# Gate and output products of a hybrid layer moved from eight plain to seven half products over two blocks

## The chip, the cores and the metric

The kernel runs on one core of a Trainium2 chip. The metric is the device time of one execution in microseconds. A core has a matrix engine (PE; its weight loads are listed as PEld), a vector engine (DVE), a scalar engine (ACT), a general engine (POOL) and a sequencer that issues the DMA transfers (SP). Each engine works through its own list of instructions in order and waits on semaphores for the others. SBUF is the on-chip memory of 128 partitions, PSUM the eight banks that PE writes, DRAM the memory behind the DMA engines.

## The reference

One layer over 2048 tokens of width 1024, all in float32:

```
xn = RMSNorm(x)
aq ak av mq mk mv mo i f ga gm = split(xn @ w_in)        # 512 each, i f 4 each, ga gm 1024 each
A = chunked band attention(aq, ak, av)                   # 2048 x 512
M = sigmoid(mo) * headnorm(mLSTM(conv(mq, mk), mv, i, f))  # 2048 x 512
y = sigmoid(ga) * (A @ w_att_proj) + sigmoid(gm) * (M @ w_mlstm_proj)
x = x + y @ w_out
x = x + relu(RMSNorm(x) @ w_up)^2 @ w_down               # 1024 -> 4096 -> 1024
out = RMSNorm(x)
```

## The kernel before

**Blocks, spans, products.** The tokens are four blocks of 512 (b = 0 to 3); two blocks make a span (s = 0, 1). Every operand of a product is split into a rounded fp32r part and a rest, and each 128 x 128 x 512 product is three matmuls (`mm3`): high x high, high x low, low x high. A weight tile holds 128 x 1024 numbers, split by one ACT copy (line 332) and one DVE subtraction (line 334) into one of three slots `wsp`; a plain tile feeds 8 such triples, 24 matmuls. The raw tile is loaded by SP into one of four `wraw` slots.

**A block, plain products.** `dense` sends 60 weight tiles per block through PE: 4 for the attention values (`evac_v`), a small product for the gates i, f (line 484), 4 for mv (`evac_mv`), then four times q, k, mq, mk, mo (`evac_q`, `evac_k`, two `evac_conv`, `evac_og`), 8 for ga (`evac_ga`), 8 times gm and the two projections together (`evac_gm`, `evac_y`), and 8 for the output product (`evac_x2`). Attention and the mLSTM recurrence (the mixers) run on all engines beside these tiles. Attention goes by heads in pairs: a pair needs four `r` slots for its q and k; a head is two units of 256 tokens (scores line 842, exponential 857, transposes 873, their split 876 and 878, the product with v on line 807, the split of the result ending on line 824). The pool `sc` holds two units, the pool `pt` the transposed tiles of one, the pool `bias` two heads.

**A span, seven half products.** After two blocks, the feed-forward layer runs over the 1024 tokens of the span by Winograd's form of Strassen's scheme: blocks of tokens are the one halving, halves of the features the other, and seven products replace eight. `quad` does one such group: seven weight tiles, each used for two output tiles, 168 matmuls on line 460, where a plain form would take 192. The weight sums that it needs are built by DVE in the first span (`quad_w`, four subtractions of 128 x 1024 a group), kept in DRAM and loaded in the second. The seven sums of the activations are made by DVE, sent to DRAM (`ud`), loaded again and split into 28 `r` slots (`take_u`, split on lines 643 and 645). `after_up` adds up the products, `spread` makes the sums for the next product, `after_down` accumulates into 16 tiles.

**Pools and order.** `r` has 28 slots of two 128 x 512 tiles, `temp` 6 tiles, `ctx` 12, `sc` 4, and four tiles hold mv. A planner written into the kernel (`Flow`) fixes the order: every piece of work is a Python generator that says what it waits for, which pool it takes from and how long it takes on which engine; the planner emits by its own clock, and prefers the lower priority number among equals. Dense products may hold at most four PSUM banks that wait for their copy:

```
        if kind == "dense":
            if room < n or pool.held + n > 4:
                return False, None
```

The instructions of an engine are then put in their last order by the tile framework, which takes the emitted order as priority and lets an instruction go ahead when what it needs is there.

The lines that the change touches are in `dense`, `loader`, `quad`'s neighbours, `attention`, `recurrence`, the evacuation functions and the pools.

Of the kernel before, what the change touches and what calls it, by code (L numbers as in the profile page):

```python
# [25 lines left out]
P = 128  # L27
# [14 lines left out]
N_W = 60  # L42
N_Q = 16
# [157 lines left out]
class Layer:  # L201
# [6 lines left out]
    def make_tiles(self, pool, psum):  # L208
# [9 lines left out]
        self.ctx = Pool([f32(f"ctx{i}", 516) for i in range(12)])  # L218
        self.mvflat = [f32(f"mv{i}", 516) for i in range(NT)]
        self.mv = [m.rearrange("p (h c) -> p h c", h=MH) for m in self.mvflat]  # L220
# [73 lines left out]
    def loader(self):  # L294
        fl, io = self.fl, self.io
        i = 0
        for s in range(NS):
            for n in range(2 * N_W):
                (raw,) = yield "get", self.wraw, 1
                fl.spawn(self.split_w(i, io["w"][n % N_W], raw), 0)  # L300
                i += 1
            for q in range(N_Q):
                if s == 0:
                    raws, evs = [], [Event() for _ in range(4)]
                    fl.spawn(self.quad_w(i, q, raws, evs), 0)
                    for n in range(4):
                        (raw,) = yield "get", self.wraw, 1
                        raws.append(raw)
                        fl.spawn(self.load_w(io["wf"][q, n], raw, evs[n]), 0)
                else:  # L310
                    wf, td = io["wf"][q], self.td[q].ap()
                    for n, src in enumerate((wf[0], wf[2], td[0], td[1], wf[3], td[2], td[3])):
                        (raw,) = yield "get", self.wraw, 1
                        fl.spawn(self.split_w(i + n, src, raw), 0)
                i += 7

    def load_w(self, src, raw, ev):
# [4 lines left out]
    def split_w(self, i, src, raw):  # L322
        yield "sp", 1750, 2000
        self.nc.sync.dma_start(raw, src)
        yield from self.split_now(i, raw)
        self.fl.put(self.wraw, raw)

    def split_now(self, i, raw):
        fl, nc = self.fl, self.nc
        (w,) = yield "get", self.wsplit, 1  # L330
# [106 lines left out]

    def quad(self, A, aev, after, release):
# [28 lines left out]
    def dense(self):  # L467
        fl = self.fl
        for b in range(NB):
            B = self.blk[b]  # L470
# [6 lines left out]
            yield from self.token_tiles(xs, xe, lambda t, bk: self.evac_v(b, t, bk))  # L477

# [8 lines left out]
            none = [None] * KT  # L487
            yield from self.token_tiles(xs, none, lambda t, bk: self.evac_mv(b, t, bk))
            self.banks.want = 2
            for j in range(4):  # L490
                for which, fn in (("q", self.evac_q), ("k", self.evac_k)):
                    (bk,) = yield from self.feature_tile(xs, none)
                    fl.spawn(fn(b, j, bk), 1)
# [3 lines left out]
            for j in range(8):  # L497
                (bk,) = yield from self.feature_tile(xs, none)
                fl.spawn(self.evac_ga(b, j, bk), 1)
            if b % 2 == 0:  # L500
                fl.spawn(self.norm_in(b + 1), 3)
            self.banks.want = 3
            for j in range(8):
                (bg,) = yield from self.feature_tile(xs, none)
                fl.spawn(self.evac_gm(b, j, bg), 1)
                (ba, bm) = yield from self.feature_tile(B["mix"], B["mix_ev"], parts=2)
                fl.spawn(self.evac_y(b, j, ba, bm), 1)
            yield "wait", B["mix_ev"]
            fl.put(self.rpool, *B["mix"], *xs)
            fl.set(B["merged"])  # L510
            if b % 2 == 1:
                s = b // 2
                U, D = self.operands(), [self.operands() for _ in range(4)]
                fl.spawn(self.take_hn_early(s, *U), 2)
                for k in range(4):
                    fl.spawn(self.take_hn_late(s, k, *U), 1)
            for j in (0, 4, 1, 5, 2, 6, 3, 7):
                (bk,) = yield from self.feature_tile(B["y"], B["y_ev"])
                fl.spawn(self.evac_x2(b, j, bk), 1)
            fl.put(self.rpool, *B["y"])  # L520
            fl.spawn(self.norm_mid(b), 2)
            if b % 2 == 0:
                continue

            self.banks.want = 0
            if b + 1 < NB:
                fl.spawn(self.norm_in(b + 1), 3)
            for i in range(8):
                yield from self.quad(*U, self.after_up(s, i), release=i == 7)
                if i == 6:  # L530
                    fl.spawn(self.take_u(s, D), 2)
            fl.spawn(self.final(s), 2)
            self.mv_left = list(self.mvflat)
# [10 lines left out]
    def norm_in(self, b):  # L544
# [43 lines left out]
        if b % 2 == 1:  # L588
            yield "wait", [self.blk[b - 1]["merged"]]
        elif b > 0:  # L590
# [35 lines left out]
    def scale_in(self, b, k, slot, bk, dst, ev):  # L626
# [9 lines left out]
        fl.set(ev)  # L636
        yield from self.split(x, dst)
        fl.put(self.ctx if b == 0 else self.sc, slot)
        fl.set(self.blk[b]["xn"][k])

    def split(self, src, dst):
        yield "act", act_ns(T)
        self.nc.scalar.copy(dst[:, 0], src)  # L643
        yield "dve", dve_ns(T)
        self.nc.vector.tensor_sub(dst[:, 1], src, dst[:, 0].bitcast(F32))  # L645


    def attention(self, b):
        fl, B = self.fl, self.blk[b]
        pt = yield "get", self.rpool, 3  # L650
        self.pt = Pool(pt)
# [3 lines left out]
        for j in range(4):  # L655
            (B["mix"][j],) = yield "get", self.rpool, 1
            if b > 0:
                (vo,) = yield "get", self.rpool, 1
                yield "sp", 900, 2000
# [12 lines left out]
        fl.put(self.rpool, *pt)  # L672
        fl.put(self.rpool, *B["v"])

    def evac_v(self, b, t, bk):
# [10 lines left out]
        if b + 1 < NB:  # L686
            yield "sp", 900, 2000
            nc.sync.dma_start(self.vdram[b].ap().bitcast(F32)[t],
                              B["v"][t].rearrange("p a c -> p (a c)").bitcast(F32))

# [39 lines left out]
    def head(self, b, h):  # L730
        fl, nc, B = self.fl, self.nc, self.blk[b]
        k, q = B["kq"][h]
        if b > 0:
            yield "sp", 900, 2000
# [18 lines left out]
        if B["heads_left"][h // 2] == 0:  # L753
            if b > 0:
                fl.put(self.rpool, B["vo"][h // 2])
            fl.set(B["mix_ev"][h // 2])
        fl.set(B["head_done"][h])

    def unit(self, b, h, u, k, q, bias, done):
# [24 lines left out]
        slots = yield "get", self.pt, len(pieces)  # L784
# [26 lines left out]
        fl.put(self.pt, *slots)  # L811
# [71 lines left out]
    def gates(self, b, bk):  # L883
        fl, nc, B, sm = self.fl, self.nc, self.blk[b], self.sm
        V = nc.vector
        (tmp,) = yield "get", self.temp, 1
# [100 lines left out]
    def recurrence(self, b):  # L987
        fl, B = self.fl, self.blk[b]
        for h in range(MH):
            B["ctx"][h] = yield "get", self.ctx, 6  # L990
            fl.set(B["ctx_ev"][h])
            fl.spawn(self.rec_head(b, h), 1)

    def evac_mv(self, b, t, bk):
        fl, nc, B = self.fl, self.nc, self.blk[b]
        if b % 2 == 0 and b > 0:
            yield "wait", [self.acc_free[b // 2 - 1]]
        yield "pool", 120
        nc.gpsimd.memset(self.mv[t][:, :, 128:129], 1.0)
        yield "act", act_ns(512, True)  # L1000
        nc.scalar.copy(self.mv[t][:, :, 0:128], bk.rearrange("p (h c) -> p h c", h=MH))
# [9 lines left out]
    def evac_conv(self, b, h, which, bk):  # L1011
        fl, nc, B = self.fl, self.nc, self.blk[b]
        yield "wait", [B["ctx_ev"][h]]
        dst = B["ctx"][h][which][:, :512]
# [34 lines left out]
    def rec_head(self, b, h):  # L1049
# [3 lines left out]
        ex, mv, cst = self.ex, self.mv, self.cst[h]  # L1053
# [30 lines left out]
        yield "wait", B["mv_ev"]  # L1084
        (hs,) = yield "get", self.hs, 1
# [49 lines left out]
        fl.set(B["mix_ev"][4 + h])  # L1135
# [15 lines left out]
    def evac_ga(self, b, j, bk):  # L1151
        fl, nc, B = self.fl, self.nc, self.blk[b]
        (g,) = yield "get", self.ctx, 1
        yield "act", act_ns(512, True)
        nc.scalar.activation(g[:, :512], bk, AF.Tanh, scale=0.5)
        fl.put_dense(self.banks, bk)
        B["ga"][j] = g
        fl.set(B["ga_ev"][j])

    def evac_gm(self, b, j, bk):  # L1160
        fl, nc, B = self.fl, self.nc, self.blk[b]
        (g,) = yield "get", self.temp, 1
        yield "act", act_ns(512, True)
        nc.scalar.activation(g[:, :512], bk, AF.Tanh, scale=0.5)
        fl.put_dense(self.banks, bk)
        B["gm"][j] = g
        fl.set(B["gm_ev"][j])

    def evac_y(self, b, j, ba, bm):
        fl, nc, B = self.fl, self.nc, self.blk[b]  # L1170
        yield "wait", [B["ga_ev"][j], B["gm_ev"][j]]
        ga, gm = B["ga"][j], B["gm"][j]
        a, m = ga[:, :512], gm[:, :512]
        yield "dve", dve_ns(512)
        nc.vector.scalar_tensor_tensor(a, a, 1.0, ba, op0=ALU.add, op1=ALU.mult)
        fl.put_dense(self.banks, ba)
        yield "dve", dve_ns(512)
        nc.vector.scalar_tensor_tensor(m, m, 1.0, bm, op0=ALU.add, op1=ALU.mult)
        fl.put_dense(self.banks, bm)
        yield "dve", dve_ns(512)  # L1180
        nc.vector.tensor_add(a, a, m)
        fl.put(self.temp, gm)
        (r,) = yield "get", self.rpool, 1
        yield "act", act_ns(512)
        nc.scalar.copy(r[:, 0], a)
        yield "dve", dve_ns(512)
        nc.vector.tensor_sub(r[:, 1], a, r[:, 0].bitcast(F32))
        fl.put(self.ctx, ga)
        B["y"][j] = r
        fl.set(B["y_ev"][j])  # L1190

    def evac_x2(self, b, j, bk):
        fl, nc, B = self.fl, self.nc, self.blk[b]
        if j == 0:
            (B["tot"],) = yield "get", self.ctx, 1
        (x,) = yield "get", self.temp, 1
        x5 = x[:, :512]
        yield "sp", 900, 2000
        nc.sync.dma_start(x5, self.io["xt"][b, j])
        yield "dve", dve_ns(512)  # L1200
        nc.vector.scalar_tensor_tensor(x5, bk, 0.5, x5, op0=ALU.mult, op1=ALU.add)
        fl.put_dense(self.banks, bk)
        kept = Event()
        fl.spawn(self.store(self.x2d[b].ap()[j], x5, kept), 1)
        (h,) = yield "get", self.ctx, 1
        yield "act", act_ns(512, False, 1)
        nc.scalar.mul(h[:, :512], x5, self.gcol[:, 1, j:j + 1])
        if b % 2 == 0:
# [485 lines left out]
```

## Time and profile before

| what | value |
|---|---|
| time, median of 3 runs | 2928.76 us (2927.49 to 2929.96) |
| time of the profiled execution | 2927.55 us |
| its span, first to last instruction | 2925.3 us |
| PE busy | 2889.1 us (99%), 13952 matmuls |
| DVE busy | 1949.4 us (67%) |
| ACT busy | 1496.0 us (51%) |
| DMA | 468.31 MB, mean 160 GB/s |

The profile is one execution; the rows give a line of the kernel, an engine, an operation, how often it ran, how long all of them kept the engine busy and the mean of one. A matmul's own duration (390 ns) contains the time it spends in the array beside the next one; how fast they follow each other is read from a stretch of time and the count of matmuls in it. The time outside the span is 2.25 us.

### The profile page before, as it was taken

To read this page: it belongs to the slowest core of one execution; us is meant where nothing else is said; L and a number is where in the kernel's file an instruction comes from. 1 tells how busy PE (TensorE), PEld (TensorE's weight loads), DVE (VectorE), ACT (ScalarE), POOL (GpSimd) and SP (SyncE) were. 2 spreads that over 40 slices of the span, in tenths; PEclk is the share of its full clock that TensorE was granted. 3 is DMA by queue.
4 is the path that set the end of the run, shared out by engine and by line. 5 is a ranking of instruction groups with operands and counts; after the bars stand their busy time and mean duration, and the time that the engine had idled before them with its cause. 6 is when DMAs were issued, how large, how long until landed. Compare 5 with 4: busy or idle time off the path is not lost.

```text
span 2925.3 us, 38512 instructions
## 1 busy us (share of the span) xinstructions
PE 2889.1 (99%) x13952; PEld 2417.2 (83%) x13952; DVE 1949.4 (67%) x3609; ACT 1496.0 (51%) x2580; POOL 53.5 (2%) x124
## 2 busy tenths in 40 slices
PE   7999999999999999999999999999999999999998
PEld 6888888888888888888888888888888888888887
DVE  5785456985585557898758854569845744468775
ACT  4664344664365556444546652456633655564444
POOL 0000000000000000000000000000000000000000
PEclk9999999999999999999999999999999999999999
DMA  5333363323465558675542234532224655587652
GB/s 170 100 93 127 112 217 120 104 72 119 138 215 206 208 209 307 232 245 194 177 157 93 89 117 123 199 101 79 64 86 141 213 187 193 196 287 233 216 177 87
DMA packets 187967, 468.31 MB, mean 160 GB/s; under 512 B 21248, under 2 KB 27520, under 8 KB 187776
## 3 DMA queue, kind: packets, MB, share of 16 engines
q1 hardware_dynamic: 187776, 465.86, 48.3%
q8 instruction: 109, 1.79, 0.3%
q14 instruction: 82, 0.67, 0.1%
HBM read 339.95 MB, written 125.83 MB: 159 GB/s over the span
## 4 chain that ended last, share of the span: by engine, by line
PE 87%; DVE 7%; ACT 2%; issue 2%; DMA 1%; POOL 0%; SPq 0%; POOLq 0%; ACTq 0%; DVEq 0%
PE bank L460 39%; PE bank L393 13%; PE bank L394 13%; PE bank L395 13%; PE bank L807 2%; PE bank L873 1%; PE bank L842 1%; DVE wsp L334 1%; DVE sc L848 1%; DVE ctx L1029 1%; ACT wsp L332 1%; ACT sc L857 1%; DVE r L645 1%; PE bank L484 1%; DVE r L878 0%
## 5 line engine op out<-in xcount | busy, mean ns | idle before, releaser
L460 PE MATMUL bank<-r,wsp 128*128 128x512 f32 x5376 | 1227.8, 390 | 2.1 <-DVE ctx L1344 1.1
L460 PEld LDWEIGHTS bank<-r,wsp 128*128 128x128 f32 x5376 | 1006.5, 188 | 213.8 <-DVE ctx L1344 2.0
L332 ACT CAST wsp<-wraw 128x1024 fp32r<-128x1024 f32 x464 | 487.9, 1051 | 742.0 <-PE bank L460 256.0
L334 DVE TENSOR_TENSOR wsp<-wraw,wsp 128x1024 fp32r<-128x1024 f32 x464 | 567.2, 1222 | 410.7 <-ACT wsp L332 406.3
L393 PE MATMUL bank<-r,wsp 128*128 128x512 f32 x1664 | 662.3, 398 | 2.7 <-DVE tmp L819 2.0
L395 PE MATMUL bank<-r,wsp 128*128 128x512 f32 x1664 | 649.1, 390 | 0.0
L394 PE MATMUL bank<-r,wsp 128*128 128x512 f32 x1664 | 648.8, 390 | 0.0
L395 PEld LDWEIGHTS bank<-r,wsp 128*128 128x128 f32 x1664 | 312.3, 188 | 67.1
L393 PEld LDWEIGHTS bank<-r,wsp 128*128 128x128 f32 x1664 | 313.0, 188 | 61.5 <-DVE tmp L819 2.8
L394 PEld LDWEIGHTS bank<-r,wsp 128*128 128x128 f32 x1664 | 313.3, 188 | 56.8
L643 ACT CAST r<-tmp 128x512 fp32r<-128x512 f32 x264 | 162.3, 620 | 125.7 <-PE bank L460 50.6
L645 DVE TENSOR_TENSOR r<-tmp,r 128x512 fp32r<-128x512 f32 x264 | 177.7, 687 | 50.7 <-ACT r L643 50.1
L857 ACT ACTIVATE sc<-sc,scs 128x640 f32<-128x640 f32 (+4 forms) x128 | 97.3, 761 | 88.7 <-DVE scs L854 84.8
L1477 DVE TENSOR_TENSOR ctx<-bank,ctx 128x512 f32<-128x512 f32 x136 | 93.1, 685 | 46.1 <-PE bank L460 45.8
L1344 DVE TENSOR_TENSOR ctx<-bank,ctx 128x512 f32<-128x512 f32 x96 | 66.2, 689 | 85.4 <-PE bank L460 84.1
L848 DVE CUSTOM_DVE_ANT_0 sc<-bank,bias 128x320 f32<-128x320 f32 (+3 forms) x240 | 102.9, 462 | 24.3 <-PE bank L842 23.7
L807 PEld LDWEIGHTS bank<-r,r 128*128 128x128 f32 x672 | 98.6, 189 | 12.6 <-DVE r L878 3.5
L807 PE MATMUL bank<-r,r 128*128 128x256 f32 (+1 forms) x672 | 105.1, 278 | 1.9 <-DVE r L878 1.9
L393 PE MATMUL bank<-wsp,r 128*128 128x512 f32 x256 | 102.9, 402 | 1.5 <-ACT r L643 1.5
L1336 ACT ACTIVATE ctx<-ctx 128x512 f32<-128x512 f32 x96 | 60.6, 632 | 83.7 <-DVE ctx L1344 83.7
L394 PE MATMUL bank<-wsp,r 128*128 128x512 f32 x256 | 100.5, 393 | 0.0
L395 PE MATMUL bank<-wsp,r 128*128 128x512 f32 x256 | 99.5, 392 | 0.0
(217 smaller groups left out, 2725.2 us busy)
## 6 DMA issues: line engine op xcount, KB each, us to landing
wraw<-in_w SPq DMA_DIRECT2D x240, 512.0 KB, 3.5
wraw<-in_wf SPq DMA_DIRECT2D x112, 512.0 KB, 3.9
tmp<-u SPq DMA_DIRECT2D x224, 256.0 KB, 3.9
wsum<-wraw SPq DMA_DIRECT2D x64, 512.0 KB, 3.1
u<-ctx SPq DMA_DIRECT2D x128, 256.0 KB, 2.4
wraw<-wsum SPq DMA_DIRECT2D x64, 512.0 KB, 3.4
u<-tmp SPq DMA_DIRECT2D x96, 256.0 KB, 2.6
sc<-in_xt SPq DMA_DIRECT2D x48, 256.0 KB, 3.2
```

Of the source, the lines that this page charges most:

```text
L332: nc.scalar.copy(w[:, 0], raw)
L334: nc.vector.tensor_sub(w[:, 1], raw, w[:, 0].bitcast(F32))
L393: mm(ps, lh, rh, start=first, stop=False)
L394: mm(ps, lh, rl, start=False, stop=False)
L395: mm(ps, ll, rh, start=False, stop=last)
L460: mm(ps, wv[:, x, k, n], a[:, y], start=new and k == 0 and x == y == 0, stop=k == 3 and x == 1, skip_group_check=True)
L643: self.nc.scalar.copy(dst[:, 0], src)
L645: self.nc.vector.tensor_sub(dst[:, 1], src, dst[:, 0].bitcast(F32))
L807: nc.tensor.matmul(bk[:, c0:c0 + w], st, sl[:, x, o:o + w], start=n == 0, stop=n == total - 1)
L848: nc.vector.tensor_tensor_reduce(out=e[:, x * w:x * w + w], in0=bks[x][:, :w], in1=br[:, j0 + x * w:j0 + x * w + w], op0=ALU.add, op1=ALU. ...
L857: nc.scalar.activation(e[:, :n], e[:, :n], AF.Exp, scale=-1.0, bias=mx, accum_out=st[:, 2:3])
L1477: nc.vector.tensor_add(a, ps, a)
```

## The change

The products for ga and gm and the output product leave the plain tiles of a block and become groups of seven half products over a span: four groups for the gates (two output quarters, each for ga and gm), two for the output product, ahead of the eight and eight of the feed-forward layer. The plain tiles of a block are then 28 (v, q and k of all heads, mv, and four times mq, mk, mo) and 8 for the two projections, which `pair_tile` does for both blocks of the span after the second block's 28 tiles. Within a block the q and k tiles of all four pairs come right behind v.

What goes with it:

- The two mixers of the even block now run beside the odd block's 28 tiles. The even block's mixed tiles go to DRAM (`mixed`) and come back for the projections (`reload_mix`); the normalized input goes to DRAM too (`xnd`) and comes back as the operand sums of the gate groups (`take_xn`). The next block's normalization (`norm_in`) starts six tiles before the end of the even block's 28.
- A projection's result is copied from PSUM to DRAM (`evac_proj`) and loaded again behind each gate tile (`after_gate`), where the gate is applied and ga's and gm's parts are added. The sums of y go through DRAM to the output groups, and those of the normalized x to the first feed-forward groups, by `spread` and `take`, as the feed-forward layer did before between its two halves.
- The 36 plain weight tiles are split once; the split pair (1 MB) is kept in DRAM (`keep_w`) and loaded in all later uses (`reload_w`), so that 108 of 144 plain tiles need no ACT and DVE work.
- The pool `ctx` has 16 tiles, and the four tiles of mv come out of it.

The core of the diff:

```
-N_W = 60
-N_Q = 16
+N_IN = 28
+N_W = 36
+N_G, N_O, N_F = 4, 2, 8
+N_Q = N_G + N_O + 2 * N_F
...
+            for h in range(2):
+                plain += [(n, 2 * s + h == 0) for n in range(N_IN)]
+            for h in range(2):
+                plain += [(n, s == 0 and h == 0) for n in range(N_IN, N_W)]
+            for n, first in plain:
+                if first:
+                    (raw,) = yield "get", self.wraw, 1
+                    fl.spawn(self.split_w(i, io["w"][n], raw, n), 0)
+                else:
+                    w = yield from self.slot_w(i)
+                    fl.spawn(self.reload_w(i, n, w), 0)
...
+    def pair_tile(self, srcs, evs):
...
+        for n in range(2):
+            got += (yield "dense", self.banks, 1)
+            for k in range(4):
...
+                self.mm3(got[-1], wv[:, 0, k, n], wv[:, 1, k, n], srcs[k][:, 0], srcs[k][:, 1], k == 0, k == 3)
...
             yield from self.token_tiles(xs, xe, lambda t, bk: self.evac_v(b, t, bk))
+            self.banks.want = 3
+            for j in range(4):
+                for fn in (self.evac_q, self.evac_k):
+                    (bk,) = yield from self.feature_tile(xs, none)
+                    fl.spawn(fn(b, j, bk), 1)
...
             for j in range(4):
-                for which, fn in (("q", self.evac_q), ("k", self.evac_k)):
...
+                if b % 2 == 0 and j == 2:
+                    fl.spawn(self.norm_in(b + 1), 3)
                 for fn in (self.evac_conv_q, self.evac_conv_k, self.evac_og):
...
-            for j in range(8):
-                (bk,) = yield from self.feature_tile(xs, none)
-                fl.spawn(self.evac_ga(b, j, bk), 1)
...
+            fl.spawn(self.reload_mix(b - 1), 1)
+            for h in range(2):
+                e = b - 1 + h
+                M = self.blk[e]
+                if h == 1:
+                    G = self.operands()
+                    for k in range(4):
+                        fl.spawn(self.take_xn(s, k, *G), 2)
+                yield "wait", [M["mix_slots"]]
+                for x in range(2):
+                    for j in range(4):
+                        bks = yield from self.pair_tile(M["mix"][4 * x:4 * x + 4], M["mix_ev"][4 * x:4 * x + 4])
+                        for n in range(2):
+                            fl.spawn(self.evac_proj(s, h, x, 2 * j + n, bks[n]), 1)
...
+            for i in range(N_G):
+                yield from self.quad(*G, self.after_gate(s, i), release=i == N_G - 1)
+                if i == N_G - 2:
+                    O = self.operands()
+                    fl.spawn(self.take(self.yd.ap(), self.y_ev[s], 0.5, *O), 2)
+            self.tots = yield "get", self.bias, 2
+            for i in range(N_O):
+                yield from self.quad(*O, self.after_out(s, i), release=i == N_O - 1)
+                if i == N_O - 2:
+                    U = self.operands()
+                    fl.spawn(self.take(self.hd.ap(), self.h_ev[s], 1.0, *U), 2)
...
+        def finish(n, which, t, ps):
...
+            nc.scalar.activation(t5, t5 if ps is None else ps, AF.Tanh, scale=0.5)
...
+            nc.sync.dma_start(a[:, :512], self.projd.ap()[2 * h + x, j])
+            yield "dve", dve_ns(512)
+            nc.vector.scalar_tensor_tensor(t5, t5, 1.0, a[:, :512], op0=ALU.add, op1=ALU.mult)
```

`spread(tiles, evs, dst, out, k)` stores a11, a12 and a22 as they come, takes three `temp` tiles once a21 is there, makes s1, s2, s4 and the last difference with four DVE operations, and gives the tiles back when all seven stores have landed. `take(src, evs, scale, A, aev)` goes through the 28 operands of a group in order (the seven sums outside, the four k tiles inside): it waits for the store, loads a `temp` tile, takes an `r` slot and splits.

644 lines of the change are left out of this document (366 added, 278 removed).

## The prediction

> **What bounds the kernel now.** I read the page first, then the busy times by stretches, then single lines. On the page:
>
> ```profile
> span 2925.3 us, 38512 instructions
> PE 2889.1 (99%) x13952; PEld 2417.2 (83%) x13952; DVE 1949.4 (67%) x3609; ACT 1496.0 (51%) x2580; POOL 53.5 (2%) x124
> PE 87%; DVE 7%; ACT 2%; issue 2%; DMA 1%; POOL 0%; SPq 0%; POOLq 0%; ACTq 0%; DVEq 0%
> L460 PE MATMUL bank<-r,wsp 128*128 128x512 f32 x5376 | 1227.8, 390 | 2.1 <-DVE ctx L1344 1.1
> L332 ACT CAST wsp<-wraw 128x1024 fp32r<-128x1024 f32 x464 | 487.9, 1051 | 742.0 <-PE bank L460 256.0
> L334 DVE TENSOR_TENSOR wsp<-wraw,wsp 128x1024 fp32r<-128x1024 f32 x464 | 567.2, 1222 | 410.7 <-ACT wsp L332 406.3
> L645 DVE TENSOR_TENSOR r<-tmp,r 128x512 fp32r<-128x512 f32 x264 | 177.7, 687 | 50.7 <-ACT r L643 50.1
> L643 ACT CAST r<-tmp 128x512 fp32r<-128x512 f32 x264 | 162.3, 620 | 125.7 <-PE bank L460 50.6
> L1344 DVE TENSOR_TENSOR ctx<-bank,ctx 128x512 f32<-128x512 f32 x96 | 66.2, 689 | 85.4 <-PE bank L460 84.1
> ```
>
> PE is the bound: 99% busy and 87% of the chain that ended last. The 464 weight splits of DVE and ACT mostly wait for PE, not the reverse. By stretches (us, then busy us and instructions of PE, PEld, DVE, ACT, POOL, clock, DMA share, GB/s): the last tiles of a block, the feed-forward groups, and the in-projection of blocks 1 and 2 with its mixers.
>
> ```profile
> 730.00:830.00 100.00, 100.00 (x443) 82.78 (x442) 57.97 (x73) 41.04 (x57) 0.00 (x0) 1.00 0.52 166
> 930.00:1030.00 100.00, 100.00 (x443) 82.81 (x442) 59.28 (x68) 53.52 (x77) 0.00 (x0) 1.00 0.56 203
> 530.00:630.00 100.00, 98.73 (x575) 86.19 (x574) 87.48 (x232) 66.25 (x142) 3.77 (x11) 1.00 0.30 93
> 1530.00:1630.00 100.00, 99.26 (x592) 87.55 (x590) 88.62 (x244) 66.31 (x148) 4.88 (x14) 1.00 0.31 98
> ```
>
> Plain tiles and half products run at the same pace: 443 matmuls in 100 us, 0.2257 us each, at full clock. So fewer matmuls are time won, if PE stays fed. It nearly always is; the price of the change is where it isn't.
>
> **The gain.** Per block, ga, gm and out take 24 plain tiles of 24 matmuls; four blocks make 2304. Per span there are now six groups of 168, for two spans 2016. The 288 that vanish are worth 288 x 0.2257 = 65.0 us. Everything else PE does stays: the projections have 384 matmuls a span in both forms.
>
> **DVE and ACT.** Weight splits fall from 464 to 344 (36 plain, 308 for groups): DVE -120 x 1.222 = -147 us, ACT -126 us. Twenty-four weight sums in the first span add some 29 us to DVE. For the 128 x 512 operations I count 264 on DVE and 188 on ACT per span now (operand splits and sums, gates, additions of products, spreads, half of the 32 projection copies), against 140 and 108: +248 x 0.69 = +171 us and +160 x 0.62 = +99 us. DVE ends near 2000 us, ACT near 1470: neither becomes a bound over the whole span. Since PE hardly waits for weight splits now, their removal itself is priced at nothing; it makes room in the in-projection.
>
> **q and k first.** These rows are block 1: v copies, q evacuations, scores (128 matmuls are 16 units of 8), unit ends, the og tiles that end the in-projection, and the last recurrence transposes.
>
> ```profile
> L681 ACT CAST r<-bank x4: 583/589/589, 433.4 to 438.5; 128x512 fp32r<-128x512 f32 x4
> L702 DVE SCALAR_TENSOR_TENSOR r<-bank,r x8: 665/684/694, 474.3 to 610.4; 64x512 fp32r<-64x512 f32 x8
> L842 PE MATMUL bank<-r,r x64: 303/309/391, 481.6 to 557.2; 128*128 128x320 f32 x64
> L842 PE MATMUL bank<-r,r x80: 303/309/391, 481.6 to 580.2; 128*128 128x320 f32 x80
> L824 ACT CAST r<-tmp x16: 399/404/412, 500.0 to 690.7; 64x256 fp32r<-64x256 f32 x16
> L1043 ACT ACTIVATE ctx<-bank x4: 592/614/628, 502.7 to 641.8; 128x512 f32<-128x512 f32 x4
> L1125 PE MATMUL bank<-const,ctx x16: 270/272/327, 530.8 to 678.4; 128*128 128x128 f32 x16
> 410.00:642.00 232.00, 230.60 (x1254) 196.31 (x1253) 172.26 (x466) 133.71 (x280) 6.06 (x17) 1.00 0.35 111
> ```
>
> Units end every (690.7 - 500.0)/15 = 12.7 us. The q/k tiles of four pairs used to come spread over 136 us (474.3 to 610.4); now eight tiles of 24 x 0.2257 = 5.42 us come in 43. The 28 `r` slots hold xs 8, pt 3, v 4 and six per pair (mix, old v, four q/k): two pairs and one slot. So pair 3's q and k wait in their banks until older q/k slots have been read for the last time. In an even block that is when the scores of units 0 to 7 are done (557.2 - 474.3 = 83 us behind the first q), in an odd block, where mix isn't given back, those of units 0 to 9 (106 us). Behind them queue the four mv banks: only four dense banks may wait, so mv's third stands. PE gets there after 12 tiles (65.0), the 16 gate matmuls (3.6), 12 of mv (2.7) and, as I estimate from the mixers' surplus below, some 20 us of theirs, at about 91 us; the first q, the fifth tile, is copied at about 29. Pair 3's banks come free at 29 + 83 + 5 = 117 or 29 + 106 + 5 = 140 us: 26 or 49 us of standing, of which a third is filled by the mixers' own matmuls (575 against 443 in 100 us, smaller ones). Idle 17 or 33 us at the old pace, 83 us for blocks 1 to 3, the upper end. The lower end is nothing: DVE loses 28 x 1.22 = 34 us of the 172 it worked in such a block, and units that end every 9 us would close the gap. I take 2 us for block 2, 7 each for blocks 1 and 3: 16 us; block 0 has shorter units and no old v: 0.
>
> **Norm of the odd block.** Its squares and loads in block 2's case:
>
> ```profile
> L566 ACT ACTIVATE sc<-sc x8: 631/632/636, 672.5 to 692.0; 128x512 f32<-128x512 f32 x8
> L564 SPq DMA_DIRECT2D sc<-in_xt x8: 327/328/382, 669.0 to 687.7; - x8
> ```
>
> 23 us from first load to last square, then the small matmuls and the scaling, some 30 us in all. It begins six tiles (33 us, with mixers about 45) ahead of need, but its `sc` slots come behind the units that wait. Attention, begun 25 us earlier than before, should end about when the 28 tiles do (before: 49 us after og). Bounds 0 and 2 x 25; I take 3, since a stand at mv gives attention time.
>
> **Projections: DMA.** The issue rows (KB each, us to landing), one row of the timeline for a hand-over between engines (0.21 us idle), and two stretches with full queues:
>
> ```profile
> wraw<-in_w SPq DMA_DIRECT2D x240, 512.0 KB, 3.5
> tmp<-u SPq DMA_DIRECT2D x224, 256.0 KB, 3.9
> u<-ctx SPq DMA_DIRECT2D x128, 256.0 KB, 2.4
> u<-tmp SPq DMA_DIRECT2D x96, 256.0 KB, 2.6
> 404.84 1.23 DVE L334 TENSOR_TENSOR wsp<-wraw,wsp 128x1024 fp32r<-128x1024 f32 x1 [0.21 <-ACT wsp L332]
> 1115.00:1135.00 20.00, 19.62 (x87) 15.96 (x86) 14.13 (x19) 15.04 (x27) 0.00 (x0) 1.00 0.90 318
> 1155.00:1175.00 20.00, 20.00 (x90) 16.55 (x89) 14.04 (x17) 5.77 (x7) 0.00 (x0) 1.00 0.90 323
> ```
>
> 16 projection tiles take PE 384 x 0.2257 = 86.7 us. In that time the first span moves, in MB: weights 4.2 raw, 8.4 kept, 8.4 loaded; mix 4.2; projection stores 8.4; xn loads 4.2; first raw gate weights 2.1: 39.9. The second span moves 35.7 (16.8 of weights loaded, none kept). A share of 0.90 at 318 to 323 GB/s makes some 355 GB/s at a full share: 112 and 101 us, 26 and 14 more than PE's. Weights run two tiles ahead (10.8 us) and half of the mix loads (6 us) can go before the stage: 26 - 17 = 9 us and nothing. Bounds 0 and 40; I take 9.
>
> The Trainium skill, "DMA: Bandwidth & Descriptors", section Bandwidth, gives 425 GB/s for a 16 MB transfer by one core alone, and its note sets an HBM limit of about 358 GB/s against that. By 425 the stage would need 94 and 84 us, so this term would be nothing and the sum 9 us lower; the trace here, at 0.90 share and 323 GB/s, lies nearer the 358.
>
> **Gates to out, out to feed-forward.** The third product of a group needs s1 of the last a21 of the group before. Chain behind the gates: tanh 0.62, gate and addition 2 x 0.69, s1 0.69, store 2.6, load 3.9, split 0.62 + 0.69, which is 10.5, eight hand-overs at 0.21 and one more store (2.4) until the neighbour's three `temp` tiles are back: 14.6 us. Cover: two products, 48 x 0.2257 = 10.8. Late by 3.8; behind out, with one operation less, by about 2.8: 13 us for two spans. DVE is full there: per span the out groups have 14 weight splits (17.1), 28 product additions (19.3), 14 additions of squares (9.6), 8 spread operations (5.5), 28 operand splits (19.2) and in the first span 8 sums (9.8): 80.5 us against 2 x 168 x 0.2257 = 75.8. The 4.7 over goes on top: 18. Bounds: 0, if the emitted order lets s1 go first, and 45 (13 + 5, doubled by transfers as slow as 0.90 share makes them, and 9 for the takes behind).
>
> **Reload of mix, take of xn.** A mix tile needs one load (a raw weight of the same size: 3.5 us) and its slot is old; the xn operands have 43 us for 28 splits and 16 sums, 30 us of DVE. Late at most by one load each: bounds 0 and 14; I take 1 us each, 4 in all. Recurrence heads now come 3 tiles apart instead of 5, with two at a time; head 3 ended 678.4 - 641.8 = 37 us after og, and 43 us of even projections stand before that is needed: nothing, and 10 if it slips. The start gets the xn stores and 1 MB stores on SP's queue; block 0's stretch is far below full share: nothing.
>
> **Sum.** -65.0 + 16 + 3 + 9 + 18 + 4 = -15. The profiled execution took 2927.55 us (2.25 outside the span), 1.2 under the median shown, so the forecast is 2912.6, rounded to 2913.
>
> **Rivals.** (1) The gain is eaten: each cost comes a third dearer than taken, 50 x 1.3 = 65, result 2922 to 2934. For it: five new places, each short; against it: the same kind of hand-over through DRAM between up and down costs PE nearly nothing today (2.1 us before 5376 matmuls on line 460). (2) Slower, by the banks held for pair 3: attention keeps its 12.7 us a unit, PE idles 83 us instead of 16 in blocks 1 to 3, 67 more: 2980. Units at 12 us or slower decide it; break-even comes at 31 us of idling. For it: the slot count and the queue of four; against it: DVE loses a fifth of its work there, and PE, while standing, runs the units' own matmuls at once. (3) Slower, by DMA: the stage pays 40 instead of 9, hand-overs 36 instead of 18: 2962. For it: 40 MB in 87 us; against it: 0.90 share with PE at 20.00 of 20 us. (4) The costs hide: nothing but 12 us of them shows, 2875. For it: PE lost little at any hand-over so far.
>
> **Chances.** A measurement of this kernel tells about 0.2%, 6 us, from no change. Forecast and near (2890 to 2922) 0.38; (4) 0.20; (1) 0.13, of which 0.09 is within 6 us and 0.04 slower; (2) 0.18; (3) 0.11. Faster 0.58, same 0.09, slower 0.33. The likeliest one's own range is 2890 to 2922; eight in ten, from (4)'s lower side to (2)'s price, 2868 to 2982.
>
> **What would show it.** Right: 13664 matmuls; 443 per 100 us in the gate groups; DVE near 2000 us; DMA some 200 MB above 468; unit ends closer than 12 us in the in-projection; PE gaps of a few us before the third product of the first out and first up group. Wrong: PE standing at mv's third bank for tens of us while line 842 runs; a DMA share above 0.9 through the projections with PE waiting for `wsp`; PE waiting for xn at the odd block's first tile.

## The result, and the profile after

The changed kernel takes 2973.66 us (median of three runs, 2971.8 to 2977.43) against 2928.76: a ratio of 1.0156 with a 95% interval of 1.0133 to 1.0179, so 45 us slower. The forecast was 2913, 15 us faster. The profiled execution of the changed kernel took 2977.43 us, 49.9 more than the one of before.

The page of the changed kernel: span, busy times, DMA, the chain that ended last, then groups of instructions and DMA issues (KB each, median us to landing):

```profile
span 2975.3 us, 38911 instructions
PE 2867.5 (96%) x13664; PEld 2380.8 (80%) x13664; DVE 1994.8 (67%) x3761; ACT 1478.9 (50%) x2620; POOL 55.7 (2%) x124
DMA packets 249891, 672.83 MB, mean 226 GB/s; under 512 B 28128, under 2 KB 34400, under 8 KB 231264
PE 80%; DVE 8%; DMA 6%; ACT 3%; issue 2%; POOL 0%; SPq 0%; POOLq 0%; DVEq 0%; ACTq 0%
L508 PE MATMUL bank<-r,wsp 128*128 128x512 f32 x7392 | 1703.9, 392 | 43.8 <-ACT r L704 18.4
L366 DVE TENSOR_TENSOR wsp<-wraw,wsp 128x1024 fp32r<-128x1024 f32 x344 | 420.1, 1221 | 238.6 <-ACT wsp L364 234.6
wsp<-wkept SPq DMA_DIRECT2D x108, 1024.0 KB, 5.7
wkept<-wsp SPq DMA_DIRECT2D x36, 1024.0 KB, 6.7
```

The 288 matmuls are gone, and DVE did not grow into a bound. But PE carries 80% of the chain where it carried 87%, DMA 6% where it was 1%, and the line of the half products (now 508, before 460) stood idle 43.8 us where it had 2.1.

Where nothing disturbs it, the pace is that of before. Stretches of the changed kernel (us; then busy us and count of PE, PEld, DVE, ACT, POOL; granted PE clock; DMA share; GB/s): the gate groups, the projections of both spans, the two out groups, the first feed-forward group, and in block 1 the 24 us behind 362:

```profile
630.00:730.00 100.00, 100.00 (x442) 82.80 (x442) 73.23 (x91) 42.50 (x59) 0.00 (x0) 1.00 0.61 211
2088.00:2188.00 100.00, 100.00 (x443) 82.78 (x442) 56.14 (x71) 40.86 (x57) 0.00 (x0) 1.00 0.61 201
501.00:596.00 95.00, 93.12 (x432) 77.11 (x431) 40.00 (x68) 31.75 (x59) 4.99 (x3) 1.00 0.91 316
1996.00:2088.00 92.00, 90.60 (x414) 74.96 (x414) 45.24 (x80) 28.43 (x54) 1.41 (x1) 1.00 0.85 286
755.00:848.00 93.00, 80.41 (x338) 64.52 (x337) 78.48 (x111) 49.24 (x73) 0.00 (x0) 0.93 0.92 322
848.00:900.00 52.00, 44.34 (x186) 34.89 (x185) 37.97 (x55) 30.74 (x51) 0.00 (x0) 0.93 0.76 277
362.00:386.00 24.00, 18.17 (x111) 15.12 (x111) 22.08 (x77) 16.99 (x42) 0.29 (x2) 0.93 0.16 47
```

443 matmuls in 100 us stand again. The out groups need 336 x 0.2257 = 75.8 us and took 93; the clock granted there was 0.93.

**An account of the whole span.** The start times of all matmuls give it: for each matmul, the time to the start of the next is set against the usual spacing of its shape (about 0.226 us for 512 columns, as in the full stretches above, 0.146 for 320, 0.118 for 256, 0.108 for 128), and what is above is a loss. A loss while the clock is granted at half, without a pause, counts as slow clock, all else as idling. The spacings themselves sum to 2856.6 us before and 2791.3 after: 65.3 less. The losses in us (in brackets the slow clock's part; "mixers" is everything ahead of the groups, before with its gate and output tiles):

| kernel | mixers, projections | gate groups | out and first up groups | other groups | sum |
|---|---|---|---|---|---|
| before | 37.6 (0) | | | 6.4 (0) | 44.0 (0) |
| after | 91.8 (10.0) | 6.9 (1.3) | 54.0 (9.7) | 6.4 (0) | 159.1 (21.0) |
| e10_held6 | 55.9 (1.4) | 15.8 (5.4) | 51.6 (7.8) | 4.6 (0) | 127.9 (14.6) |
| e7_qk2 | 53.7 (3.5) | 10.4 (0) | 53.3 (9.1) | 6.1 (0) | 123.5 (12.6) |
| e3_direct | 86.1 (3.3) | 5.7 (1.6) | 8.8 (0) | 5.1 (0) | 105.7 (4.9) |
| e4_resplit | 76.8 (6.4) | 1.7 (0) | 53.6 (8.1) | 6.6 (0) | 138.7 (14.5) |
| e11_all_held6 | 50.4 (0) | 0.8 (0) | 8.5 (0) | 8.7 (0) | 68.4 (0) |

Losses grew by 115.1, the gain was 65.3: 49.8 us, which is the difference of the two profiled executions. So two places lose some 54 us each: the blocks with their mixers, and the hand-overs behind the gate groups and the out groups.

### The profile page after: what moved, and what is told of

The parts are those of the page before. It is cut to its first block, busy times and chain, and to the rows that moved or that the text cites. A ratio compares the mean times of both kernels' runs of the same rounds, so it can differ in the third digit from the quotient of the medians.

```text
span 2975.3 us, 38911 instructions
## 1 busy us (share of the span) xinstructions
PE 2867.5 (96%) x13664; PEld 2380.8 (80%) x13664; DVE 1994.8 (67%) x3761; ACT 1478.9 (50%) x2620; POOL 55.7 (2%) x124
## 3 DMA queue, kind: packets, MB, share of 16 engines
q8 instruction: 107, 1.75, 0.2%
## 4 chain that ended last, share of the span: by engine, by line
PE 80%; DVE 8%; DMA 6%; ACT 3%; issue 2%; POOL 0%; SPq 0%; POOLq 0%; DVEq 0%; ACTq 0%
PE bank L508 50%; PE bank L425 7%; PE bank L426 7%; PE bank L427 7%; PE bank L919 2%; PE bank L954 2%; PE bank L985 1%; DMA tmp<-u 1%; DMA tmp<-hn 1%; DVE sc L960 1%; DMA tmp<-y 1%; DVE wsp L366 1%; DVE r L707 1%; DMA ctx<-xn 1%; DVE r L990 1%
## 5 line engine op out<-in xcount | busy, mean ns | idle before, releaser
L508 PE MATMUL bank<-r,wsp 128*128 128x512 f32 x7392 | 1703.9, 392 | 43.8 <-ACT r L704 18.4
L508 PEld LDWEIGHTS bank<-r,wsp 128*128 128x128 f32 x7392 | 1392.8, 189 | 344.6 <-ACT r L704 19.7
L366 DVE TENSOR_TENSOR wsp<-wraw,wsp 128x1024 fp32r<-128x1024 f32 x344 | 420.1, 1221 | 238.6 <-ACT wsp L364 234.6
L364 ACT CAST wsp<-wraw 128x1024 fp32r<-128x1024 f32 x344 | 361.7, 1052 | 418.1 <-PE bank L508 359.5
L425 PE MATMUL bank<-r,wsp 128*128 128x512 f32 x896 | 361.8, 404 | 0.0
L427 PE MATMUL bank<-r,wsp 128*128 128x512 f32 x896 | 350.9, 392 | 0.0
L426 PE MATMUL bank<-r,wsp 128*128 128x512 f32 x896 | 350.3, 391 | 0.0
L702 ACT CAST r<-tmp 128x512 fp32r<-128x512 f32 x280 | 171.3, 619 | 128.7 <-PE bank L508 55.5
L707 DVE TENSOR_TENSOR r<-tmp,r 128x512 fp32r<-128x512 f32 x280 | 187.2, 687 | 57.0 <-ACT r L702 56.8
L427 PEld LDWEIGHTS bank<-r,wsp 128*128 128x128 f32 x896 | 168.5, 188 | 36.8
L425 PEld LDWEIGHTS bank<-r,wsp 128*128 128x128 f32 x896 | 169.2, 189 | 29.8 <-DVE r L990 0.8
L426 PEld LDWEIGHTS bank<-r,wsp 128*128 128x128 f32 x896 | 169.2, 189 | 29.1
L1629 DVE TENSOR_TENSOR ctx<-bank,ctx 128x512 f32<-128x512 f32 x192 | 131.7, 686 | 78.7 <-PE bank L508 78.4
L1323 DVE TENSOR_TENSOR ctx<-bank,ctx 128x512 f32<-128x512 f32 x144 | 98.8, 688 | 88.3 <-PE bank L508 88.3
L1315 ACT COPY ctx<-bank 128x512 f32<-128x512 f32 x144 | 83.8, 582 | 68.1 <-PE bank L508 68.1
```

The costliest lines, as they stand in the source:

```text
L364: nc.scalar.copy(w[:, 0], raw)
L366: nc.vector.tensor_sub(w[:, 1], raw, w[:, 0].bitcast(F32))
L425: mm(ps, lh, rh, start=first, stop=False)
L426: mm(ps, lh, rl, start=False, stop=False)
L427: mm(ps, ll, rh, start=False, stop=last)
L508: mm(ps, wv[:, x, k, n], a[:, y], start=new and k == 0 and x == y == 0, stop=k == 3 and x == 1, skip_group_check=True)
```

## The experiments

The ideas to be told apart: A, the q and k tiles of four pairs ahead of mv hold banks that wait for `r` slots, and PE stands; B, the hand-overs through DRAM (spread, store, load, split) come later than two products cover; and beside them the load that the kept weights put on DMA.

**The hand-overs.** e2_old_operands gives the out groups and the first feed-forward groups operands that are ready long before, of the same number and kind (it leaves out the sums that those groups should use).

```diff
-                    fl.spawn(self.take(self.yd.ap(), self.y_ev[s], 0.5, *O), 2)
+                    fl.spawn(self.take(Old(self.xnd[2 * s].ap()), self.old(s), 0.5, *O), 2)
...
-                    fl.spawn(self.take(self.hd.ap(), self.h_ev[s], 1.0, *U), 2)
+                    fl.spawn(self.take(Old(self.xnd[2 * s].ap()), self.old(s), 1.0, *U), 2)
```

> The changed kernel, but the output groups and the first feed-forward groups take the normalized input of the span's first block (in DRAM long before) in place of the sums of y and of the normalized x; stores, loads, splits and all other work stay. So the products out and up use other numbers. Theory B (the hand-over of the last sums through DRAM costs PE its gaps and cold clock): some 50 us less, 2915 to 2930 us. Rival C (DVE and the DMA queues are overfull there, whoever waits): the gaps stay in good part, 2950 us or more.

Measured: 2948.75 us, ratio 1.0071 [1.0051, 1.0092], 25 us back, about half of what was lost there and between the two expectations. The out groups of the first span fell from a loss of 16.8 to 2.1 us, but its first up group lost 16.8 instead of 12.3. There PE now waits for an ACT copy (line 1326) until a DVE step of `spread` (line 1382) is done, which has read a `ctx` tile. That step runs at 859.5 us, right behind operand splits that waited until 858.1 for a load issued at 850.9. So operands that do not hang on the last sums give back half of this loss. The largest piece of what is left stands behind a slow load again, by way of the queues of ACT and DVE, which work in order. Waits in that stretch of e2_old_operands, those of PE and then those ahead of it (us in total, times, longest):

```profile
PE bank L516 <- ACT ctx L1326: 12.7, 2, 9.8
...
ACT r L713 <- DMA tmp<-xn: 6.8, 8, 2.2
DVE r L718 <- ACT r L713: 5.1, 3, 1.8
...
ACT ctx L1326 <- DVE tmp L1382: 1.5, 1, 1.5
```

e3_direct takes the trip through DRAM away where it is late: the sums of the last quarter (k = 2 and 3) are split straight from SBUF into their `r` slots, with no store and no load, and their tiles are free after the split.

```diff
+        def send(m, x):
+            if direct is None:
+                fl.spawn(self.store(dst[m, k], x, out[m][k]), 1)
+            else:
+                A, aev, scale = direct
+                fl.spawn(self.take_split(x, m, k, A, aev, scale), 1)
...
-        fl.spawn(self.store(dst[2, k], s1, out[2][k]), 1)
+        send(2, s1)
```

> The changed kernel with the last quarter's sums (k = 2 and 3) of y and of the normalized x split straight from SBUF into r slots, without store and load; DVE and ACT do the same work, 28 stores and 28 loads a span fall out. Theory B: the chain shrinks by about 7 us, below the 10.8 us of cover; the gaps behind gates and out nearly go, 2920 to 2935 us. Rival C (DVE full): 2955 us or more.

Measured: 2929.14 us, ratio 1.0004 [0.9995, 1.0014]: 45 us back, level with the kernel before. This shortens the chain and takes 28 stores and 28 loads a span off the queues at once; e2_old_operands, which keeps all transfers, shows that at least 25 us of it are the operands. PE's waits before and after this cure, first of the changed kernel in the two out stretches, then of e3_direct from 745 to 835 us:

```profile
PE bank L508 <- ACT r L704: 9.9, 1, 9.9
PE bank L508 <- ACT r L704: 8.5, 1, 8.5
```

```profile
PE bank L508 <- DVE ctx L1462: 3.4, 3, 1.5
```

Line 704 is the ACT half of the operand split with a scale. The chain of the changed kernel up to the first of these waits (start us, length, what) shows what stood ahead of it:

```profile
754.42 0.60 DVE ctx L1417
...
756.75 1.22 DVE wsp L366
757.97 0.60 DVE ctx L1409
758.57 1.14 DVE wraw L396
...
769.19 0.60 DVE tmp L1371
769.79 0.07 DVE wraw L406
...
771.54 0.38 SPq L341
...
772.02 0.42 SPq L1503
...
772.49 5.59 DMA y<-tmp
...
778.14 4.44 DMA tmp<-y
...
782.60 0.64 ACT r L704
783.24 0.04 issue
783.28 6.90 PE bank L508 x17
```

The last product of the gates leaves PE at 754.8. DVE needs until 769.8 for the last s1 (line 1371), since gates (1409, 1417), weight splits (366), weight sums (396), operand splits and the other quarter's sums stand in its queue. SP sends the store of s1 at 772.5: ahead of it in SP's queue are a raw weight load (341), which goes out at 771.0 when DVE ends a weight sum (406), and another store. Then come 5.6 us of store and 4.4 us of load. From the last product of the gates to the one that waited it is 28.5 us, against 10.8 us of cover.

**q and k first.** e1_qk_by_head puts the q and k tiles of each pair back with the mq, mk and mo tiles of the same j, behind mv. e7_qk2 moves only pairs 2 and 3. e10_held6 leaves the order and lets dense products hold six waiting banks.

```diff
-            for j in range(4):
-                for fn in (self.evac_q, self.evac_k):
...
-                for fn in (self.evac_conv_q, self.evac_conv_k, self.evac_og):
+                for fn in (self.evac_q, self.evac_k, self.evac_conv_q, self.evac_conv_k, self.evac_og):
```

> The changed kernel with one part undone: q and k of a pair come again with mq, mk, mo of the same j, behind mv. Theory A (pair 3's q and k hold banks, the plain products stand behind mv's third bank; 24 us without plain matmuls in blocks 1 and 3): the stand goes, 2940 to 2955 us. Rival (the mixers then end after the 28 tiles, and the odd block's normalization and the projections wait for them): 2975 to 3010 us.

```diff
-            for j in range(4):
+            for j in range(2):
                 for fn in (self.evac_q, self.evac_k):
...
+                if j < 2:
+                    for fn in (self.evac_q, self.evac_k):
+                        (bk,) = yield from self.feature_tile(xs, none)
+                        fl.spawn(fn(b, j + 2, bk), 1)
```

> The changed kernel with only pairs 0 and 1 of q and k ahead of mv; those of pairs 2 and 3 come behind the mq, mk and mo tiles of j = 0 and 1. Theory A (the third and fourth pair find no slots while the first two are in use): no more than two pairs need their slots early, so the stand ahead of mv goes: 2943 to 2953 us, what putting all q and k back gave (2947.7) or a few us better, with the hand-overs unchanged. Rival (the loss is in having q and k early at all): less than a third of the 26 us, 2965 or more.

```diff
-            if room < n or pool.held + n > 4:
+            if room < n or pool.held + n > 6:
```

> The changed kernel with one number altered: dense products may hold six PSUM banks that wait for their copy instead of four. Theory A (PE stands in blocks 1 to 3 because pair 3's q and k and the mv tiles behind them use up the four waiting banks): two more tiles of 24 matmuls (10.8 us of work) go through before the stand, in each of three blocks, so up to 32 us come back unless the mixers lack those banks: 2945 to 2960 us, and the stretch 362 to 386 us of block 1 is no longer free of plain matmuls. Rival (the mixers themselves, not the banks, set the pace of those blocks; PE would stand all the same, only later): within 6 us of the changed kernel's 2973.7, or slower, because the mixers' own products then wait for one of the two banks that are left.

Measured: 2947.74 (ratio 1.0067 [1.0052, 1.0082]), 2943.34 (1.0057 [1.004, 1.0074]) and 2944.76 us (1.0057 [1.0042, 1.0072]): 26 to 30 us back each, with the hand-overs as before. One number in the planner gives the same as the other order of tiles, so it is the banks. The stretch 362 to 386 us of block 1, in the changed kernel by lines of PE (the first three rows; no row of the plain tiles' lines 425 to 427 is among the six), then in e7_qk2:

```profile
L919 PE MATMUL bank<-r,r 128*128 128x256 f32 (+1 forms) x40 | 8.5, 326 | 4.1 <-DVE r L990 3.7 <-ACT r L988 0.2
L954 PE MATMUL bank<-r,r 128*128 128x320 f32 x30 | 7.4, 349 | 0.3 <-DVE r L788 0.3
L985 PE MATMUL bank<-const,sc 128*128 128x128 f32 x33 | 5.2, 279 | 0.1
```

```profile
L425 PE MATMUL bank<-r,wsp 128*128 128x512 f32 x22 | 9.2, 418 | 0.0
L426 PE MATMUL bank<-r,wsp 128*128 128x512 f32 x22 | 8.6, 393 | 0.0
L427 PE MATMUL bank<-r,wsp 128*128 128x512 f32 x22 | 8.6, 391 | 0.0
```

For 24 us only the mixers' products run, 103 of the 111 of them attention's (lines 919, 954 and 985), and they wait for DVE and ACT steps of their own; block 3 has the same from 1855 us. The busy row of these 24 us with six waiting banks, where the changed kernel had 18.17 us and 111 matmuls:

```profile
362.00:386.00 24.00, 24.00 (x132) 20.85 (x131) 17.74 (x54) 15.65 (x34) 0.29 (x2) 1.00 0.54 181
```

**Kept weights.** e4_resplit loads and splits the plain weights anew at each use, as before.

```diff
-                if first:
+                if True:
                     (raw,) = yield "get", self.wraw, 1
-                    fl.spawn(self.split_w(i, io["w"][n], raw, n), 0)
+                    fl.spawn(self.split_w(i, io["w"][n], raw), 0)
```

> The changed kernel with its plain weights loaded raw and split in every use, as before the change; nothing is kept in DRAM. DMA moves some 90 MB less, DVE works 132 us and ACT 113 us more. If the traffic of the kept weights costs time (projection stage, hand-overs): 2955 to 2970 us. If DVE's room in the in-projection is worth what theory A needs (units come faster): 2985 to 3010 us. If both hide: 2970 to 2980 us.

Measured: 2954.61 us, ratio 1.0089 [1.0072, 1.0106]: 19 us back, just below the range for a traffic that costs time, though DVE and ACT have 108 weight splits more. 12.7 us of it are in block 0 (losses of 22.7 and 10.0 us by the account above), where all weights are split in both kernels and only the stores are gone. The issues from 19 to 237 us, of the changed kernel with the busy row of block 0, then of e4_resplit with its own:

```profile
wkept<-wsp SPq DMA_DIRECT2D x28, 1024.0 KB, 6.8
wraw<-in_w SPq DMA_DIRECT2D x27, 512.0 KB, 4.6
19.00:251.00 232.00, 223.45 (x1158) 187.52 (x1158) 172.10 (x473) 134.33 (x301) 12.25 (x32) 0.97 0.79 281
```

```profile
wraw<-in_w SPq DMA_DIRECT2D x30, 512.0 KB, 3.5
19.00:237.00 218.00, 214.10 (x1151) 180.60 (x1151) 172.79 (x474) 135.16 (x301) 13.31 (x32) 1.00 0.48 156
```

Block 0 takes 14 us more when 28 MB of stores run through it. Whether that comes by the slower transfers (4.6 against 3.5 us) or by the `wsp` slots that the stores hold was not separated. Nor is it a fixed price: in the other order of tiles, by the same account to within 1 us, block 0 loses 16 us with the stores (e6, below) and 18 without them (e8).

**The cures together.** Four kernels join edits that stand above: e5_direct_qk2 (e3 and e7), e6_direct_qk_by_head (e3 and e1), and both again with the split of e4.

> e3 (direct split of the last quarter's sums, 2929) and q and k of two pairs only ahead of mv; pairs 2 and 3 follow behind mq, mk, mo of j = 0 and 1. Theory A (pair 3's banks) is a separate cost from theory B: the 26 us of e1 come off e3 in full or more, 2898 to 2906 us. If both cure the same stands: 2915 us or more.

> e3 and e1 together (q and k of a pair with mq, mk, mo of the same j). Separate costs: 2929 - 26 = 2903, 2898 to 2910 us; attention starts later than in e5, so e5 should be some us faster if the mixers' end matters, equal if not.

> e6 and, as in e4, no weights kept in DRAM (each plain tile split in every use). If the kept weights' traffic costs what e4 gained wherever the rest stands: 2903 - 15 = 2888, 2880 to 2895 us. If e4 only relieved the hand-overs that e3 has already cured: within 5 us of e6; if DVE's room counts once the stands are gone: slower than e6.

> e5 and no weights kept in DRAM. Same alternatives as for the run before, against e5: 2880 to 2895 us if the traffic of the kept weights is the cost, within 5 us of e5 or slower if not.

Measured: e5 2900.43 us (0.9903 [0.9889, 0.9918]), e6 2901.37 (0.9910 [0.9895, 0.9924]), e8 2898.27 (0.9898 [0.9882, 0.9915]), e9 2892.31 (0.9880 [0.9866, 0.9895]). A's and B's losses lie in different places and add up. The kept weights cost only 3 us (no more than the spread of the two kernels' runs) and 8 us once the other two are cured. By the same account, projections and gate groups together lose 18 us in e6 and 6 in e8, 17 in e5 and 7 in e9; in e8 the four blocks lose 8 us more, so little of it is left. By what was expected, e8 (within 5 us of e6) speaks against the traffic as the cost and e9 (in the range for it) for it: the two orders of tiles do not agree. e11_all_held6 is e9 with six waiting banks:

> The kernel with the three cures together (last quarter's sums split straight from SBUF, pairs 2 and 3 of q and k later, weights split again at each use; 2892.3 us), and besides six waiting banks instead of four. If the later pairs and the two banks cure the same stand, the banks find nothing left to give: 2889 to 2896 us, and the time in which PE idles in the in-projections stays near 49 us. Rival (two different losses that happened to be of one size): another 10 to 25 us faster, 2867 to 2882. Losing more than 6 us would mean that the mixers miss the two banks: 2898 or more.

Measured: 2886.67 us, ratio 0.9856 [0.9839, 0.9872], faster than both kernels. The banks gave 5.6 us more, a little beyond what was expected of one and the same stand and far from another 25: later pairs and more banks cure mostly the same loss. Its page:

```profile
span 2884.6 us, 38987 instructions
PE 2827.3 (98%) x13664; PEld 2363.0 (82%) x13664; DVE 2112.9 (73%) x3890; ACT 1561.1 (54%) x2707; POOL 56.0 (2%) x124
```

So 41 of the half products' 65 us show once the losses are down to 68.4 us, 24 above those of before; the way in which the change fed them had lost the gain.

## Why the prediction was wrong, step by step

**The gain** was right: 65.0 taken, 65.3 found, 13664 matmuls, 443 in 100 us in the gate groups. **DVE and ACT** too: 2000 and 1470 us forecast, 1994.8 and 1478.9 measured, neither a bound.

**Gates to out, out to feed-forward** is the step that failed most: 18 us taken, 54 measured (its own upper bound was 45), 45 of them given back by e3_direct. The place and the chain were right (a third product that waits for its operand). The sizes were not. The chain took 28.5 us where 14.6 was reckoned: the store and the load 5.6 and 4.4 us instead of 2.6 and 3.9, which are the medians of a whole execution; 15.0 us of DVE's queue instead of some 3; and 2.7 us of SP's queue, which the sum did not have. The step saw that DVE is full (80.5 us of work in 75.8) but charged only the surplus of 4.7; what stands in an engine's queue ahead of a late operand delays it even where the sum over the stage would fit. And this chain is not the whole loss: with operands that were ready long before (e2_old_operands) about half stayed, most of it at the first up group of the first span, where a copy that needs a `ctx` tile comes late. The step had reckoned a wait for tiles at the `temp` tiles alone, at 2.4 us.

**q and k first**: 16 us taken, 26 to 30 given back by each of three edits. Rival 2 named the mechanism, banks held for pair 3 with mv queued behind, and it came to pass, in blocks 1 and 3 above all. Its condition was wrong: it was to need units of 12 us, and 9 were to close the gap. The units did end every (441.7 - 307.3)/15 = 9.0 us in block 1 of the changed kernel (ends of the units; copies of pairs' q):

```profile
L936 ACT CAST r<-tmp x16: 401/404/414, 307.3 to 441.7; 64x256 fp32r<-64x256 f32 x16
L771 DVE SCALAR_TENSOR_TENSOR r<-bank,r x8: 665/688/694, 281.2 to 378.5; 64x512 fp32r<-64x512 f32 x8
```

Block 1 starts at 251 us. The last q was copied 127 us later (140 forecast for the old pace), PE came to its stand after 109 us (about 91 forecast): at 9 us a unit the two came nearer, but did not meet. What the prediction named as a sign of being wrong, PE standing for tens of us while the scores run, is the 26 us from 361 to 387 us without a plain product. Block by block e7_qk2 takes 6.8, 14.7, 5.1 and 12.4 us off the losses, where 0, 7, 2 and 7 had been put; so the step was too small by half, and wrong in calling block 0 free. Some of these 39 us come back as losses in the gate groups (10.4 and 15.8 us in e7_qk2 and e10_held6 instead of 6.9).

**1 MB stores in block 0** were priced at nothing, since that stretch was "far below full share". It has a share of 0.79, and without the stores block 0 of this kernel is 12.7 us better, though not in the order of e6 and e8. Keeping the weights was a change in the wrong direction for the time: e4_resplit, which takes only this part back, is 19 us faster.

**Projections: DMA**: 9 taken, but the stage lost 2.7 and 2.1 us. The share went to 0.91 as forecast, and PE still had 93.12 us of 95. Over these 95 us at 316 GB/s 30.0 MB moved, not 39.9: a quarter of it ran earlier or later than was reckoned. The traces do not decide between the 425 and the 358 GB/s that the Trainium skill gives ("DMA: Bandwidth & Descriptors", section Bandwidth): 316 at 0.91 is 347 at a full share, below both, while the 11 us from 2256 us, at a share of 1.05, moved 376 GB/s, between the two. Part of the price stands one stage later: the gate groups lose 6.9 us, but 1.7 and 0.8 in e4_resplit and e11_all_held6, which keep no weights. Rival 3 fails with this stage, though its doubled hand-overs (36) fell short of the 54.

**Norm of the odd block** (3) and **reload and take** (4) stayed small: at the first products of block 3 PE waited once for an operand, 1.1 us, and in the first gate groups once for a sum of xn, 2.8 us. They were not measured alone.

In all 50 us of losses were forecast and 115 came. The time lies between rivals 2 and 3, by rival 2's mechanism and a hand-over loss larger than rival 3's. The slow clock, 21 of the 115, was in no step of the sum.

## What to carry to other kernels

A hand-over through DRAM costs what its transfers and its engine's queue take in that very stretch; read them there, not from the kernel's mean, and where the last part of a stage feeds the first of the next, keep that part in SBUF. When a piece of work is moved ahead, ask for which slots it will wait and what is queued behind the banks that it holds: here one limit of the planner, four to six, was worth 29 us. And work for which nobody waits is not worth a transfer to save it: keeping the split weights cost 19 us here, and 3 and 8 where the other losses were cured.

## What the runs showed of the hardware

**The clock halves without an idle window.** Before, the granted clock is half only at the end of the span; after, there are 14 further spells of it, 68 us in all. All lie on one grid of 3.41 us and last one to four of its steps. In a spell matmuls of 512 columns start every 427 ns instead of 226. Five stretches of the changed kernel: three steps ahead of a spell, the spell behind the third, and the one in which PE waited 9.9 us for its operand:

```profile
109.60:113.00 3.40, 1.35 (x8) 0.83 (x6) 3.27 (x6) 1.97 (x4) 0.46 (x2) 1.00 0.83 209
372.40:375.80 3.40, 1.84 (x10) 1.17 (x10) 3.27 (x12) 3.30 (x8) 0.00 (x0) 1.00 0.39 121
2335.10:2338.50 3.40, 2.27 (x14) 1.66 (x13) 1.52 (x4) 0.91 (x3) 0.00 (x0) 1.00 1.00 343
...
2338.50:2341.90 3.40, 2.99 (x7) 2.41 (x8) 1.22 (x3) 0.36 (x1) 0.00 (x0) 0.50 1.02 357
...
775.20:788.80 13.60, 5.52 (x12) 4.09 (x13) 4.71 (x8) 5.14 (x8) 0.00 (x0) 0.50 0.93 321
```

PE was never idle for a whole step ahead of these three spells; in the third it was busy for 2.27 of 3.4 us. Over all steps of that grid from 20 us on, each of the nine at full clock with at most 1.45 us of busy PE (0.09, 0.52, 0.69, 0.84, 1.19, 1.19, 1.33, 1.37, 1.45) was followed by half clock. Of those in between, the ones with 1.75, 1.86, 2.17, 2.30, 2.42 and 2.51 us were, others with 1.64, 1.68, 1.84 and 2.08 were not; above 2.6 none was. The traces of all the other runs agree: up to 1.46 us of busy PE always, above 2.45 never. The Trainium skill, "TensorE: Matmul & The Clock Gate", Part 1, tells of a free-running window of about 3.4 us and of half clock after at least one idle window. The grid agrees with it; that the window must be idle does not, and the measurement decides: a window that is half filled can do. A spell of one step costs some 1.6 us (3.41 x (1 - 226/427)) beside the gap that brought it. e3_direct, which closes the gaps at the hand-overs, has 4.9 us of slow clock instead of 21.0, and e11_all_held6 none; no run changed the clock alone.

**Transfers slow down together before the share is full.** The same 256 KB store and load of y, from 596 to 755 us, where the share is 0.64, and from 765 to 785 us at 0.95 (KB each, median us to landing):

```profile
y<-tmp SPq DMA_DIRECT2D x6, 256.0 KB, 2.3
tmp<-y SPq DMA_DIRECT2D x9, 256.0 KB, 2.9
...
y<-tmp SPq DMA_DIRECT2D x3, 256.0 KB, 5.7
tmp<-y SPq DMA_DIRECT2D x7, 256.0 KB, 5.7
```

Both take about twice as long, and it is this time that stands in the chain for which PE waits. These are few transfers, and the seven loads went out close behind each other; what slows them was not separated.
